# RWKV-7 units of a two-layer decoder trunk: state as a block-diagonal tile, triangular inverse from 64x64 tiles, uninterrupted r and v products

## The chip, the cores and the metric

The kernel runs on one core of a Trainium2 chip. The metric is device time in microseconds, as the median of the timed runs. All times of a trace are microseconds from the start of the span of one profiled execution, durations of single instructions are also given in ns. PE is TensorE, DVE is VectorE, ACT is ScalarE, POOL is GpSimd, SP is the queue that issues most DMAs.

## The reference, cut to what matters

A trunk of two layers on 256 tokens of 1024 features. The first layer is RWKV-7 time mixing and a dense SwiGLU; the second is dilated attention and a mixture of eight experts. The change touches only the time mixing. There, each of 16 heads carries a state of 64x64, and the recurrence over the tokens is

```python
def step(state, inp):
    r_t, w_t, k_t, v_t, a_t, b_t = inp
    sa = jnp.einsum('bhvk,bhk->bhv', state, a_t)
    state = state * w_t[:, :, None, :] + sa[..., None] * b_t[:, :, None, :] + v_t[..., None] * k_t[:, :, None, :]
    return state, jnp.einsum('bhvk,bhk->bhv', state, r_t)
```

with `r`, `k`, `v` from projections of the modulated input, and a per-head norm, a bonus term and a gate behind it, then the output projection `w_out`. Everything is float32.

## The kernel before, in words

**Chunks and units.** The 256 steps of the recurrence are cut into four chunks of 64 tokens. Within a chunk the recurrence becomes matrix products and the inverse of a 64x64 triangular matrix per head; between chunks only the state goes on. A *unit* (function `unit`, line 866) is one token tile of 128 tokens (two chunks, called `ch`) and four heads, so there are eight units: `c_` is the group of four heads, `t` the token tile. Four *lanes* hold the tiles of four units at a time, and each lane has one PSUM bank of its own (`lps`, line 880). The unit of `t = 1` needs the state that the unit of `t = 0` of the same heads leaves.

**What a unit does, in order.** Decay, keys and their norms (from line 908); transposes into `ART`, `BKn`, `BKT`; products that give `SM`, where `SM[:, ch, h, 0:64]` is what the inverse starts from; the inverse `E` (from line 1016); the chunk loop (from line 1089); head norm, bonus, gate and a transpose into `yg`, which the output projection reads.

**The inverse.** It doubles the block size at each of four levels (2, 4, 8, 16): product of `SM` with `T`, copy of it to `X` on ACT, product of `X` with `E`, a predicated copy into `E` on DVE, and a 32x32-blocked transpose of `E` into `T` on DVE. The two chunks lie in partitions 0 to 63 and 64 to 127. So that one product serves both chunks, `SM` is copied into `SMA`, a tile of 128x128 per head with the two 64x64 blocks on its diagonal, and `X` is such a tile too; POOL sets the other blocks to zero, and ACT writes the two blocks in two copies. A last level works on 32x32 tiles.

**The chunk loop.** For each chunk: `U` from `SM` times `SV` plus `ART` times the state; `E` times `U` into `SV`; the new state from `BKn` and `SV`, scaled by `PC` on DVE; `Y` from `SM` times `SV` plus `ART` times the state. The state is a tile `[128, 2, 64]`: of a pair of heads, one lies in partitions 0 to 63, the other in 64 to 127, so the product with the state is one of 64 rows of weights for each head, and the products with `SM` (128 rows of weights) and with the state alternate head by head.

**r and v.** `rv_task` (line 1189) makes r and v of four heads in *pieces*: four row chunks, two token tiles, and three products (`mm3`, line 452) for each, 24 products in all. There are 16 pieces. It hands control back ahead of every triple.

**What sets the order.** The order of the instructions on PE, DVE, ACT and POOL is written out by a planner (`spin`, line 1320): every task yields the engine and the tiles that its next instructions need, and the planner, by its own estimates of costs, always issues the one that can begin first. Between two yields nothing else is put. `keep_clock` (line 1358) adds products of nothing (`identr`) where the planner's ledger of columns says that PE does too little. All engine instructions pass through one helper, so all carry its line, L190; groups are told apart by tile names. On each engine they then run in the order written. Two further tasks run beside the units on ACT and POOL: rows of the adaLN weights are scaled (`rawa`) and summed (`acc`).

Of the kernel before, what the change touches and what calls it, by code (L numbers as in the profile page):

```python
# [33 lines left out]
S = 256  # L34
# [7 lines left out]
RANK0 = 1000                                              # ranks count from -RANK0  # L42
# [49 lines left out]
def tile_kernel(ctx: ExitStack, tc: tile.TileContext, cst_d, att_d, x, c, ada_w, ada_b, ln_g, ln_b, mu, w_rkv,  # L92
# [18 lines left out]
    def load(t_, src):  # L111
        """a large load into a tile of a ring"""
        n = 1
        for d_ in t_.shape:
            n *= d_
        k = t_.tensor.name
        clk["DMA"] = max(clk["DMA"], free.get(k, 0.0)) + n * 4 / 360
        rdy[k] = clk["DMA"] + 2000
        (nc.gpsimd if k in by_gp else SY).dma_start(t_, src)
# [5 lines left out]
    past = []                                              # when columns went through the tensor engine, and how many  # L125

    class Engine:
        """an engine, with an estimate of the time of every instruction, by which the units are interleaved"""
# [43 lines left out]
        def __getattr__(self, op):  # L172
            fn = getattr(self.real, op)

            def call(*a, **kw):
# [3 lines left out]
                for r in aps:  # L179
                    start = max(start, rdy.get(r.tensor.name, 0.0))  # L180
                    if r.tensor.name[:3] in ("psb", "mmb") and self.nm != "PE":    # one engine after the other
                        start = max([start] + [v for k, v in psr.get(r.tensor.name, {}).items() if k != self.nm])
# [49 lines left out]
    def raw_at(j, shape):  # L232
        """the place's tile, or its two tiles of half the size"""
# [9 lines left out]
    def raw_load(rws, src, rows_=None):  # L243
        """src: [128, k, n]"""
# [10 lines left out]
    def raw_tiles(kk, n):  # L255
        """for one load: a place, or two places of half the size, which are used once"""
# [34 lines left out]
    tl = cp.tile([128, 1], F32, name="tl")                # has the table of the next functions loaded  # L291
# [11 lines left out]
    # ---- adaLN vectors  # L303
    mods = {}

    def ada_end(idx, ps):
        """ps[g * 32]: a quarter of the vector"""
# [13 lines left out]
    def ada_pe(idx, get_raw, get_ps, n):  # L321
        """one adaLN vector; mods[idx][p, k] = vector[k * 128 + p]. Four groups of columns of the tensor engine
        each sum a quarter of the columns"""
# [17 lines left out]
    def ada_sum(idx, acc, get_ps):  # L341
        """sum over the partitions"""
# [15 lines left out]
    def ada_task(idx):  # L358
        """background work: one adaLN vector, chunk by chunk"""
# [17 lines left out]
    def ada_lane(idx):  # L377
        """the same beside the units"""
# [40 lines left out]
    def bcast_steps(idx, o, get_ps):  # L419
        """mods[idx] along the free axis, the same on every partition"""  # L420
# [17 lines left out]
    # ---- small helpers  # L438
# [21 lines left out]
    def wstream(w, K, n0, n, fine=False):  # L460
        """yield (k, hi, lo) for every 128 rows of w[:K, n0:n0+n]; fine: the last load by row chunks"""
# [15 lines left out]
    def proj2(xh, xl, w, K, n0, n, first=False, mid=()):  # L477
        """two token tiles, n <= 512 columns; first: all of token tile 0 before token tile 1"""
# [21 lines left out]
    def proj_wide(xh, xl, w, K, last=4, stream=None, mid=(), late=None):  # L500
        """[256, K] @ [K, 1024]; the last few row chunks finish token tile 0 before token tile 1"""
# [26 lines left out]
    def ln_rsqrt(var):  # L528
        """sqrt(1 / (var + eps)) per partition"""
# [14 lines left out]
    def pn_norm(t, yps, gate1, u, sc=()):  # L544
        """u = normalised sum of the residual and the gated branch, of token tile t; yps[half]: [128, 512]"""
# [26 lines left out]
    def pn_mod(t, u, mods, get_ps, get_tmp):  # L572
        """mods: (A, B, sink(t, hf, tmp)) per modulated copy, transposed"""
# [18 lines left out]
    def pn_res(t, u, gb, bb, eng):  # L592
        """the new residual"""
# [26 lines left out]
    # =====================================================================================  # L620
    # layer 0: RWKV-7
    # =====================================================================================
    up = rw_stack.enter_context(tc.tile_pool(name="up", bufs=2, reuse_waits="tile"))       # units
# [50 lines left out]
    # Work is cut into tasks, which are interleaved. A task yields what its next instructions begin with:  # L674
    # (engine, tiles read) or a condition to wait for.
# [6 lines left out]
    def loader():  # L682
        """weights, two tiles ahead"""
# [94 lines left out]
    def rvvar_task(i):  # L778
        """the variants of x for r and v, hi and lo"""
# [13 lines left out]
    # low-rank branches, first stage (transposed outputs)  # L793
# [43 lines left out]
    # units of one token tile (two chunks of 64) and four heads; a lane holds the tiles of one unit.  # L837
# [5 lines left out]
    def row_tiles(c_):  # L843
        """the broadcast rows of four heads"""
# [21 lines left out]
    def unit(i, lane):  # L866
# [25 lines left out]
        def newton(v, nm):  # L892
            """sqrt(1 / v)"""
# [18 lines left out]
        # decay, in-context rate a = (1 + tanh) / 2, keys; the sigmoids enter by their tanh  # L912
# [17 lines left out]
        # k2 = 2 * k * (1 + (a - 1) * k_a)  # L930
# [85 lines left out]
        # E = transpose of the inverse of (1 - strictly lower part of A B), by doubling the block size  # L1016
# [5 lines left out]
        SMA = lt("SMA", "BS", (128, 4, 128))  # L1022
        yield GP,
        halves(lambda sl, ch: GP.memset(SMA[sl, :, 64 - ch * 64:128 - ch * 64], 0.0))
        yield SC, SM
        halves(lambda sl, ch: SC.copy(SMA[sl, :, ch * 64:ch * 64 + 64], SM[sl, ch, :, 0:64]))
        X = lt("X", "t34", (128, 4, 128))
        yield GP,
        halves(lambda sl, ch: GP.memset(X[sl, :, 64 - ch * 64:128 - ch * 64], 0.0))
# [7 lines left out]
        for b in (2, 4, 8, 16):  # L1037
            yield PE, SMA, T
            ps = lps((128, 4, 64))
            for h in range(4):  # L1040
                PE.matmul(ps[:, h], SMA[:, h], T[:, h], start=True, stop=True)
            yield SC, ps
            halves(lambda sl, ch: SC.copy(X[sl, :, ch * 64:ch * 64 + 64], ps[sl]))
            yield PE, X
            ps = lps((128, 4, 64))
            for h in range(4):
                PE.matmul(ps[:, h], X[:, h], E[:, h], start=True, stop=True)
# [7 lines left out]
        for ch in range(2):  # L1055
            s0, s1 = slice(ch * 64, ch * 64 + 32), slice(ch * 64 + 32, ch * 64 + 64)
            for h in range(4):
# [8 lines left out]
        for ch in range(2):  # L1066
            s0, s1 = slice(ch * 64, ch * 64 + 32), slice(ch * 64 + 32, ch * 64 + 64)
            for h in range(4):
# [20 lines left out]
        # chunk after chunk; U = E'(A S + (strictly lower part of A K) V), its place in SV holds zeros before  # L1089
        Y = l4("Y", "t5")  # L1090
        for ch in range(2):
            sl = slice(ch * 64, ch * 64 + 64)
            yield lambda: ST_n.get(c_, 0) >= t * 2 + ch
            st = ST.get(c_)
            for par in range(2):
                hs = slice(par * 64, par * 64 + 64)
                yield PE, SV
                ps = lps((128, 2, 64))
                for pr in range(2):
                    h = pr * 2 + par  # L1100
                    PE.matmul(ps[sl, pr], SM[:, ch, h, 0:64], SV[:, ch, h * 64:(h + 1) * 64], start=True,
                              stop=st is None)
                    if st is not None:
                        PE.matmul(ps[sl, pr], ART[hs, pr, ch, 0], st[hs, pr], start=False, stop=True)
                yield SC, ps
                SC.copy(U[sl, par::2], ps[sl])
# [6 lines left out]
            if not (t == 1 and ch == 1):  # L1113
                yield PE, SV
                ps2 = lps((128, 2, 64))
                for h in range(4):
                    pr, hs = h // 2, slice((h % 2) * 64, (h % 2) * 64 + 64)
                    PE.matmul(ps2[hs, pr], BKn[:, ch, h * 64:(h + 1) * 64], SV[:, ch, h * 64:(h + 1) * 64],
                              start=True, stop=True)
                yield V, ps2  # L1120
                sn = up.tile([128, 2, 64], F32, name=f"ST{c_ % 2}_{ch}", bufs=1)
                pcb = PC[:, :, ch:ch + 1].to_broadcast([128, 2, 64])
                if st is None:
                    V.tensor_tensor(sn, ps2, pcb, op=OP.mult)
                else:
                    V.tensor_tensor(sn, ps2, st, op=OP.add)
                    yield V, sn
                    V.tensor_tensor(sn, sn, pcb, op=OP.mult)
                ST[c_] = sn
                ST_n[c_] = t * 2 + ch + 1  # L1130
            for par in range(2):
                hs = slice(par * 64, par * 64 + 64)
                yield PE, SV
                ps = lps((128, 2, 64))
                for pr in range(2):
                    h = pr * 2 + par
                    PE.matmul(ps[sl, pr], SM[:, ch, h, 64:128], SV[:, ch, h * 64:(h + 1) * 64], start=True,
                              stop=st is None)
                    if st is not None:
                        PE.matmul(ps[sl, pr], ART[hs, pr, ch, 1], st[hs, pr], start=False, stop=True)  # L1140
                yield SC, ps
# [1104 lines left out]
```

## Time and profile before

| what | value |
|---|---|
| median of three timed runs | 1970.92 us (1966.15, 1970.92, 1975.42) |
| span of the profiled execution | 1977.1 us |
| what the profile gives for that execution beside its span | nothing; the span itself stands 6.2 us above the median |
| instructions | 25695 |
| busy share of PE, DVE, ACT, POOL | 94%, 77%, 60%, 21% |
| mean granted TensorE clock | 0.915 |

One of the 40 slices of the page is 49.4 us. The units run from about 103 us to 495 us, in slices 3 to 10; the dense SwiGLU follows until about 705 us, attention until about 960 us, and the experts fill the rest. A group's "busy" is the union of its instructions' durations. [...] A float32 product leaves two records, each with its own load of weights; a product of the split weights (`whi`, `wlo`) leaves one.

### The profile page before, as it was taken

The page shows a single profiled execution, that of the slowest core. Times are in us where ns is not written, and L with a number is a line of the kernel's source. Part 1 is how long each engine was busy: PE and PEld are TensorE (multiplying, and loading weights), DVE is VectorE, ACT ScalarE, POOL GpSimd, SP SyncE. Part 2 cuts the span into 40 slices and gives each one's busy share as a digit, 9 for nine tenths or more (in the row PEclk, how much of TensorE's full clock was granted, in tenths as well). Part 3 has the DMA queues.
Part 4 walks back from the last instruction along what each step waited for, and adds up shares of the span by engine and source line. Part 5 has one row for each costly group of instructions (what it writes and reads, how often), then busy time and mean ns, then how long its engine had stood idle before and what let it go on. Part 6 is the DMA issues. An engine that isn't in the chain of part 4 may idle for free. (4 is left out here: it accounts for less than half of the span.)

```text
span 1977.1 us, 25695 instructions
## 1 busy us (share of the span) xinstructions
PE 1861.9 (94%) x9345; PEld 1491.3 (75%) x9345; DVE 1527.9 (77%) x2033; ACT 1184.5 (60%) x1592; POOL 408.3 (21%) x333
## 2 busy tenths in 40 slices
PE   5889999999999978898899999999999999999996
PEld 2478778887687866666788888888878878788775
DVE  3893347444798776786889989898898888988888
ACT  2354344333455536663678777787777777777764
POOL 2743324230345237753100000000000000000110
PEclk8895558559899989998999999999999999999998
DMA  8542213212498946654789999999999999999990
GB/s 279 153 139 64 67 57 98 92 64 72 165 331 305 332 143 234 232 192 174 294 299 344 364 348 347 376 343 364 337 349 353 355 350 337 354 348 355 342 318 25
DMA packets 213562, 498.89 MB, mean 252 GB/s; under 512 B 14634, under 2 KB 28818, under 8 KB 213428
## 3 DMA queue, kind: packets, MB, share of 16 engines
q1 hardware_dynamic: 212564, 494.03, 70.3%
q0 software_dynamic: 864, 3.15, 0.4%
q8 instruction: 75, 1.23, 0.3%
q14 instruction: 59, 0.48, 0.1%
HBM read 496.07 MB, written 1.06 MB: 251 GB/s over the span
## 5 line engine op out<-in xcount | busy, mean ns | idle before, releaser
L190 DVE TENSOR_TENSOR wlo<-raw,whi 128x1024 fp32r<-128x1024 f32 x804 | 999.7, 1281 | 144.2 <-ACT whi L190 130.2
L190 ACT CAST whi<-raw 128x1024 fp32r<-128x1024 f32 x812 | 828.1, 1048 | 263.3 <-PE mmb L190 207.0
L190 PE MATMUL mmb<-wlo,xeh 128*128 128x512 f32 x896 | 356.4, 398 | 4.9 <-DVE wlo L190 4.1
L190 PE MATMUL mmb<-whi,xeh 128*128 128x512 f32 x896 | 353.1, 395 | 0.0
L190 PE MATMUL mmb<-whi,xel 128*128 128x512 f32 x896 | 351.8, 393 | 0.0
L190 PEld LDWEIGHTS mmb<-wlo,xeh 128*128 128x128 f32 x896 | 168.7, 188 | 47.1 <-DVE wlo L190 13.4
L190 POOL TENSOR_TENSOR macc<-macc,gate 128x1024 f32<-128x1024 f32 x2 | 5.7, 2890 | 925.3 <-ACT gate L190 925.3
L190 PEld LDWEIGHTS mmb<-whi,xeh 128*128 128x128 f32 x896 | 168.6, 188 | 34.3 <-ACT whi L190 0.2
L190 PEld LDWEIGHTS mmb<-whi,xel 128*128 128x128 f32 x896 | 168.7, 188 | 32.7
L190 PE MATMUL psb<-wlo,ah 128*128 128x512 f32 x448 | 176.6, 394 | 1.5 <-DVE wlo L190 1.5
L190 PE MATMUL psb<-whi,al 128*128 128x512 f32 x448 | 174.8, 390 | 0.0
L190 PE MATMUL psb<-whi,ah 128*128 128x512 f32 x448 | 161.9, 392 | 0.0
L190 POOL TENSOR_TENSOR acc<-acc,raw 128x512 f32<-128x512 f32 (+1 forms) x62 | 128.2, 2082 | 75.6 <-DVE acc L190 44.2
L190 POOL TENSOR_TENSOR acc<-acc,rawa 128x512 f32<-128x512 f32 x56 | 74.2, 1330 | 142.2 <-ACT rawa L190 81.2
L190 PEld LDWEIGHTS psb<-wlo,ah 128*128 128x128 f32 x448 | 84.1, 188 | 24.7 <-DVE wlo L190 6.2
L190 PEld LDWEIGHTS psb<-whi,ah 128*128 128x128 f32 x448 | 83.5, 188 | 18.8 <-ACT whi L190 1.6
L190 PEld LDWEIGHTS psb<-whi,al 128*128 128x128 f32 x448 | 84.1, 188 | 16.5
L190 PE MATMUL mmb<-whi,f_xl 128*128 128x512 f32 (+1 forms) x192 | 72.5, 378 | 2.1 <-DVE f_xl L190 2.1
L190 PE MATMUL mmb<-whi,f_xh 128*128 128x512 f32 (+1 forms) x192 | 73.0, 381 | 0.0
L190 PE MATMUL mmb<-wlo,f_xh 128*128 128x512 f32 (+1 forms) x192 | 72.5, 377 | 0.2 <-DVE wlo L190 0.2
L190 ACT CAST ah<-psb 128x512 fp32r<-128x512 f32 x56 | 32.7, 583 | 61.0 <-PE psb L190 60.8
L190 ACT COPY X<-psb 64x256 f32<-64x256 f32 (+1 forms) x80 | 27.5, 344 | 64.1 <-PE psb L190 63.0
(415 smaller groups left out, 3048.3 us busy)
## 6 DMA issues: line engine op xcount, KB each, us to landing
raw<-in_moe_w_gu_dram SPq DMA_DIRECT2D x192, 1024.0 KB, 6.5
raw<-in_moe_w_down_dram SPq DMA_DIRECT2D x83, 1024.0 KB, 6.1
raw<-in_moe_w_gu_dram SPq DMA_DIRECT2D x60, 512.0 KB, 7.0
raw<-in_moe_w_down_dram SPq DMA_DIRECT2D x56, 512.0 KB, 6.1
raw<-in_ada_w_dram SPq DMA_DIRECT2D x42, 512.0 KB, 5.2
rawa<-in_ada_w_dram SPq DMA_DIRECT2D x40, 512.0 KB, 3.6
raw<-in_ada_w_dram SPq DMA_DIRECT2D x15, 1024.0 KB, 7.2
raw<-in_rw_w_rkv_dram SPq DMA_DIRECT2D x24, 512.0 KB, 3.7
```

The lines of the kernel that those rows point to most:

```text
L190: return fn(*a, **kw)
```

## The change

In the inverse, `SMA` and the wide `X` go. Each of the eight 64x64 matrices of a level (four heads, two chunks) is a product of its own, by the helper `mm64` that was there already, in the order head by head with the two chunks alternating; `X` is written in one copy. In the last level the two loops change places, so that the chunks alternate there too.

The state becomes `[128, 2, 128]`: of each pair of heads a 128x128 tile with the heads' states on the diagonal and zeros elsewhere. POOL makes `pcm`, the decay of the chunk in that layout with zeros off the diagonal (a memset and two copies for each unit), and DVE scales with it. The product with the state is one for each pair, and follows all four products with `SM`. `U` and `Y` come out in one copy each. The state of the first chunk lies in the lane's tile `t1`, that of the second in a tile of its own. The wait for the state of the unit before stands behind the four products with `SM`, no longer ahead of them.

In `rv_task` the 24 products of a piece follow one another with no yield between them.

The rest of the diff removes comments. Its core:

```diff
-        SMA = lt("SMA", "BS", (128, 4, 128))
-        yield GP,
-        halves(lambda sl, ch: GP.memset(SMA[sl, :, 64 - ch * 64:128 - ch * 64], 0.0))
-        yield SC, SM
-        halves(lambda sl, ch: SC.copy(SMA[sl, :, ch * 64:ch * 64 + 64], SM[sl, ch, :, 0:64]))
-        X = lt("X", "t34", (128, 4, 128))
-        yield GP,
-        halves(lambda sl, ch: GP.memset(X[sl, :, 64 - ch * 64:128 - ch * 64], 0.0))
...
         for b in (2, 4, 8, 16):
-            yield PE, SMA, T
+            yield PE, SM, T
             ps = lps((128, 4, 64))
-            for h in range(4):
-                PE.matmul(ps[:, h], SMA[:, h], T[:, h], start=True, stop=True)
+            mm64(ps, lambda sl, ch, h: SM[sl, ch, h, 0:64], lambda sl, ch, h: T[sl, h])
             yield SC, ps
-            halves(lambda sl, ch: SC.copy(X[sl, :, ch * 64:ch * 64 + 64], ps[sl]))
+            X = l4("X", "t1")
+            SC.copy(X, ps)
             yield PE, X
             ps = lps((128, 4, 64))
-            for h in range(4):
-                PE.matmul(ps[:, h], X[:, h], E[:, h], start=True, stop=True)
+            mm64(ps, lambda sl, ch, h: X[sl, h], lambda sl, ch, h: E[sl, h])
...
+        pcm = lt("pcm", "t34", (128, 2, 2, 128))
+        yield GP, PC
+        GP.memset(pcm.rearrange("p c r n -> p (c r n)"), 0.0)
+        halves(lambda sl, par: GP.tensor_copy(
+            pcm[sl, :, :, par * 64:par * 64 + 64],
+            PC[sl].rearrange("p r c -> p c r").unsqueeze(3).to_broadcast([64, 2, 2, 64])))
+
+        def with_state(ps, sl, ch, a, st):
+            for pr in range(2):
+                PE.matmul(ps[sl, 2 * pr:2 * pr + 2].rearrange("p h n -> p (h n)"), ART[:, pr, ch, a], st[:, pr],
+                          start=False, stop=pr == 1)
...
-            for par in range(2):
-                hs = slice(par * 64, par * 64 + 64)
-                yield PE, SV
-                ps = lps((128, 2, 64))
-                for pr in range(2):
-                    h = pr * 2 + par
-                    PE.matmul(ps[sl, pr], SM[:, ch, h, 0:64], SV[:, ch, h * 64:(h + 1) * 64], start=True,
-                              stop=st is None)
-                    if st is not None:
-                        PE.matmul(ps[sl, pr], ART[hs, pr, ch, 0], st[hs, pr], start=False, stop=True)
-                yield SC, ps
-                SC.copy(U[sl, par::2], ps[sl])
+            for h in range(4):
+                PE.matmul(ps[sl, h], SM[:, ch, h, 0:64], SV[:, ch, h * 64:(h + 1) * 64], start=h == 0,
+                          stop=first and h == 3)
+            st = None
+            if not first:
+                yield lambda: ST_n.get(c_, 0) >= t * 2 + ch
+                st = ST[c_]
+                yield PE, st
+                with_state(ps, sl, ch, 0, st)
+            yield SC, ps
+            SC.copy(U[sl], ps[sl])
...
-                ps2 = lps((128, 2, 64))
-                for h in range(4):
-                    pr, hs = h // 2, slice((h % 2) * 64, (h % 2) * 64 + 64)
-                    PE.matmul(ps2[hs, pr], BKn[:, ch, h * 64:(h + 1) * 64], SV[:, ch, h * 64:(h + 1) * 64],
-                              start=True, stop=True)
+                ps2 = lps((128, 2, 128))
+                for pr in range(2):
+                    prs = slice(pr * 128, (pr + 1) * 128)
+                    PE.matmul(ps2[:, pr], BKn[:, ch, prs], SV[:, ch, prs], start=True, stop=True)
...
+            yield lambda: xvn[i] > q * 4 + 3
+            yield PE, hi, lo, xl, ps[0], ps[1]
             for k in range(4):
                 kk = q * 4 + k
                 for t in range(2):
-                    yield lambda: xvn[i] > kk
-                    yield PE, hi, lo, xl, ps[t]
```

More of the change, by code (lines that the diff above doesn't have):

```diff
@@ L1054, in unit @@
         ps = lps((128, 4, 32))
-        for ch in range(2):
-            s0, s1 = slice(ch * 64, ch * 64 + 32), slice(ch * 64 + 32, ch * 64 + 64)
-            for h in range(4):
+        for h in range(4):
+            for ch in range(2):
+                s0, s1 = slice(ch * 64, ch * 64 + 32), slice(ch * 64 + 32, ch * 64 + 64)
                 PE.matmul(ps[s1, h], SM[s0, ch, h, 32:64], T[s0, h, 0:32], start=True, stop=True,
@@ L1065, in unit @@
         ps = lps((128, 4, 32))
-        for ch in range(2):
-            s0, s1 = slice(ch * 64, ch * 64 + 32), slice(ch * 64 + 32, ch * 64 + 64)
-            for h in range(4):
+        for h in range(4):
+            for ch in range(2):
+                s0, s1 = slice(ch * 64, ch * 64 + 32), slice(ch * 64 + 32, ch * 64 + 64)
                 PE.matmul(ps[s0, h], X[s1, h, 0:32], E[s1, h, 32:64], start=True, stop=True,
@@ L1090, in unit @@
         Y = l4("Y", "t5")
+        pcm = lt("pcm", "t34", (128, 2, 2, 128))
[8 more added lines that the diff above has]
+                          start=False, stop=pr == 1)
         for ch in range(2):
             sl = slice(ch * 64, ch * 64 + 64)
-            yield lambda: ST_n.get(c_, 0) >= t * 2 + ch
-            st = ST.get(c_)
-            for par in range(2):
-                hs = slice(par * 64, par * 64 + 64)
-                yield PE, SV
-                ps = lps((128, 2, 64))
-                for pr in range(2):
-                    h = pr * 2 + par
-                    PE.matmul(ps[sl, pr], SM[:, ch, h, 0:64], SV[:, ch, h * 64:(h + 1) * 64], start=True,
-                              stop=st is None)
-                    if st is not None:
-                        PE.matmul(ps[sl, pr], ART[hs, pr, ch, 0], st[hs, pr], start=False, stop=True)
-                yield SC, ps
-                SC.copy(U[sl, par::2], ps[sl])
+            first = t == 0 and ch == 0
+            yield PE, SV
+            ps = lps((128, 4, 64))
+            for h in range(4):
+                PE.matmul(ps[sl, h], SM[:, ch, h, 0:64], SV[:, ch, h * 64:(h + 1) * 64], start=h == 0,
[8 more added lines that the diff above has]
+            SC.copy(U[sl], ps[sl])
             yield PE, U
@@ L1114, in unit @@
                 yield PE, SV
-                ps2 = lps((128, 2, 64))
-                for h in range(4):
-                    pr, hs = h // 2, slice((h % 2) * 64, (h % 2) * 64 + 64)
-                    PE.matmul(ps2[hs, pr], BKn[:, ch, h * 64:(h + 1) * 64], SV[:, ch, h * 64:(h + 1) * 64],
-                              start=True, stop=True)
-                yield V, ps2
-                sn = up.tile([128, 2, 64], F32, name=f"ST{c_ % 2}_{ch}", bufs=1)
-                pcb = PC[:, :, ch:ch + 1].to_broadcast([128, 2, 64])
@@ L1123, in unit @@
-                if st is None:
-                    V.tensor_tensor(sn, ps2, pcb, op=OP.mult)
-                else:
+                ps2 = lps((128, 2, 128))
+                for pr in range(2):
+                    prs = slice(pr * 128, (pr + 1) * 128)
+                    PE.matmul(ps2[:, pr], BKn[:, ch, prs], SV[:, ch, prs], start=True, stop=True)
+                yield V, ps2
+                sn = lt("ST", "t1", (128, 2, 128)) if ch == 0 else up.tile([128, 2, 128], F32, name=f"ST{c_ % 2}",
+                                                                                   bufs=1)
@@ L1126, in unit @@
+                if st is not None:
                     V.tensor_tensor(sn, ps2, st, op=OP.add)
                     yield V, sn
-                    V.tensor_tensor(sn, sn, pcb, op=OP.mult)
+                V.tensor_tensor(sn, ps2 if st is None else sn, pcm[:, ch], op=OP.mult)
                 ST[c_] = sn
                 ST_n[c_] = t * 2 + ch + 1
[L1131 to L1141, printed above, removed]
-                SC.copy(Y[sl, par::2], ps[sl])
+            yield PE, SV
@@ L1144, in unit @@
+            ps = lps((128, 4, 64))
+            for h in range(4):
+                PE.matmul(ps[sl, h], SM[:, ch, h, 64:128], SV[:, ch, h * 64:(h + 1) * 64], start=h == 0,
+                          stop=first and h == 3)
+            if not first:
+                with_state(ps, sl, ch, 1, st)
+            yield SC, ps
+            SC.copy(Y[sl], ps[sl])
         yield GP, v_, bon
```

## The prediction

> **What bounds the kernel now.** I read the page's slices first, then the engines' busy time by stage, then the waits of the units' stage, then its timeline on PE. On the page, PE's busy tenths and the granted clock:
>
> ```profile
> PE   5889999999999978898899999999999999999996
> PEclk8895558559899989998999999999999999999998
> ```
>
> PE is at 9 and over in slices 4 to 6, 8 and 9 while its clock is at about half. So the clock, not idle time, marks the stage. The stretches of the units (length; busy time with count of PE, PEld, DVE, ACT, POOL; clock; DMA share; GB/s):
>
> ```profile
> 151.00:291.00 140.00, 139.35 (x766) 114.96 (x766) 48.20 (x146) 54.46 (x132) 41.70 (x51) 0.51 0.20 60
> 291.00:349.00 58.00, 54.94 (x390) 46.72 (x390) 43.77 (x121) 29.34 (x69) 22.37 (x29) 0.86 0.34 105
> 349.00:435.00 86.00, 85.79 (x444) 72.64 (x444) 41.05 (x116) 29.75 (x72) 27.62 (x33) 0.51 0.22 73
> 435.00:495.00 60.00, 59.56 (x423) 43.54 (x423) 29.98 (x75) 22.19 (x51) 5.39 (x11) 0.99 0.24 80
> ```
>
> They hold two cold stretches, 140 + 86 = 226 us, in which PE is never free, the clock is 0.51, DVE and ACT are busy under half the time and DMA under a quarter. There PE's work is time, one for one. In 291 to 349 DVE is busy 43.77 of 58 us, so PE does not bound that stretch alone. The waits from 125 to 495 agree: the others wait for PE.
>
> ```profile
> DVE E L190 <- PE psb L190: 67.0, 26, 7.1
> ACT X L190 <- PE psb L190: 63.0, 30, 5.3
> ```
>
> Nothing behind the stage has a start of its own: DMA stands at 0.24 when the stage ends, and the dense layer's loads wait for buffers that the units hold. So I take what is won by 495 as won at the end.
>
> **The change part by part.** Prices come from starts on PE's timeline, at half clock:
>
> ```profile
> 199.66 1.97 PE L190 MATMUL psb<-E,X 128*128 128x64 f32 x8
> 201.55 1.11 PE L190 MATMUL psb<-U,E 64*64 64x64 f32 x8
> 202.59 0.58 PE L190 MATMUL mmb<-whi,x2h 128*128 128x256 f32 x1
> 202.97 0.41 PE L190 MATMUL mmb<-wlo,x2h 128*128 128x256 f32 x1
> ...
> 204.81 0.70 PE L190 MATMUL psb<-SV,BKn 128*64 128x64 f32 x8
> 205.44 1.97 PE L190 MATMUL psb<-T,SMA 128*128 128x64 f32 x8
> 207.17 0.56 PE L190 MATMUL mmb<-whi,x2h 128*128 128x256 f32 x1
> ...
> 208.09 0.48 PE L190 MATMUL psb<-SV,SM 128*64 128x64 f32 x2
> ...
> 211.31 0.47 PE L190 MATMUL psb<-E,X 128*128 128x64 f32 x1
> ```
>
> and at full clock:
>
> ```profile
> 445.67 0.68 PE L190 MATMUL psb<-U,E 64*64 64x64 f32 x8
> 446.27 1.10 PE L190 MATMUL psb<-T,SMA 128*128 128x64 f32 x8
> 447.31 0.45 PE L190 MATMUL psb<-SV,BKn 128*64 128x64 f32 x8
> 447.69 0.50 PE L190 MATMUL mmb<-whi,ygh 128*128 128x512 f32 x1
> ...
> 478.53 0.33 PE L190 MATMUL psb<-SV,SM 128*64 128x64 f32 x2
> ...
> 479.04 0.33 PE L190 MATMUL psb<-SV,SM 128*64 128x64 f32 x2
> ```
>
> How much of each kind lies in the first and in the second cold stretch (records by form; busy, mean ns):
>
> ```profile
> L190 PE MATMUL psb<-E,X 128*128 128x64 f32 x104 | 25.5, 427 | 0.0
> L190 PE MATMUL psb<-ST,ART 64*64 64x64 f32 x72 | 17.1, 339 | 0.0
> L190 PE MATMUL mmb<-whi,x0h 128*128 128x256 f32 x13 | 6.4, 491 | 0.0
> L190 PE MATMUL mmb<-whi,x2h 128*128 128x256 f32 x9 | 4.5, 505 | 0.0
> ...
> L190 PE MATMUL psb<-E,X 128*128 128x64 f32 x56 | 13.0, 421 | 0.2 <-ACT X L190 0.2
> L190 PE MATMUL psb<-ST,ART 64*64 64x64 f32 x48 | 11.4, 339 | 0.0
> L190 PE MATMUL mmb<-whi,x2h 128*128 128x256 f32 x16 | 8.2, 515 | 0.0
> L190 PE MATMUL mmb<-whi,x0h 128*128 128x256 f32 x5 | 2.4, 484 | 0.0
> ```
>
> *Inverse.* One of its products for four heads leaves 8 records and costs 1.73 us (205.44 to 207.17) to 1.89 us (199.66 to 201.55) cold, 1.04 warm (446.27 to 447.31). Afterwards it is 8 products in alternating quadrants, 16 records. No such pair is in the trace. Its bounds: U,E, one quadrant throughout, leaves 8 records in 1.04 cold and 0.60 warm, so 16 cost at most 2.08 and 1.20; SV,BKn, which alternates the two column halves, leaves 8 in 0.63 and 0.38, so 16 cost 1.26 and 0.76 with two entries, less with one. I take 1.1 and 0.65, by SV,BKn, the nearer kind: its neighbouring products share no cell of the array either. There are 8 units x 4 levels x 2 = 64 such groups. Of E,X 104 + 56 = 160 records are cold, 20 groups; T,SMA comes once for each, so 40 are cold and 24 not. Cold: 40 x (1.8 - 1.1) = 28 us off; elsewhere 24 x 0.39 = 9 off. At the other bound it is 40 x 0.28 = 11 and 24 x 0.16 = 4 more instead.
>
> *U and Y.* Four heads with the state cost 3.22 cold (208.09 to 211.31) and four times 0.51 = 2.04 warm (478.53 to 479.04 is one head), since each head goes from 128 rows of weights to 64 and back. Afterwards there are four products with SM in a row, priced as U,E, and two of 128 columns with the state, 4 records, for which I take these, of 128x128 weights and 128 columns, as nearest:
>
> ```profile
> 434.85 1.89 PE L190 MATMUL mmb<-cst,mod 128*128 128x128 f32 x8
> 436.58 0.67 PE L190 MATMUL psb<-E,X 128*128 128x64 f32 x5
> ```
>
> 1.73 / 8 = 0.216 each cold, half that warm. New: 1.04 + 0.86 = 1.90, and 0.60 + 0.43 = 1.03. Twenty-four groups have the state, of which (72 + 48) / 8 = 15 are cold: 15 x 1.32 = 20 off; elsewhere 9 x 1.01 = 9 off. If the SM products went at the pace of column halves (0.63), 26 off; if they kept 0.40 a pair, 15 x 0.76 = 11.
>
> *Pieces.* A product that follows other work costs 0.38 (202.59 to 202.97), against 0.21 inside a run. The mean durations of the first of a triple, 484 to 515 ns, stand some 0.09 over the 0.41 of the second. With 13 + 9 + 16 + 5 = 43 triples cold that is 4 us, of which one entry in eight stays: 3 off.
>
> *Small PE items.* The state product of BKn becomes 4 records of 0.216 in place of 8 in 0.63: 9 times 0.23, 2 more. The last level's alternation can at best halve a group of 32x32 products; 1.5 off.
>
> Cold sum: 28 + 20 + 3 - 2 + 1.5 = 50. Elsewhere 9 + 9 = 18, of which I count half, as DVE shares that time: 9. Together **59**.
>
> *The clock.* In 291 to 349 it comes back after runs of r and v products:
>
> ```profile
> 313.60:317.00 3.40, 3.40 (x16) 3.22 (x15) 3.29 (x5) 0.94 (x1) 3.27 (x5) 0.50 0.00 0
> 317.00:320.40 3.40, 3.16 (x25) 2.82 (x25) 3.32 (x11) 2.87 (x9) 0.07 (x1) 1.00 0.58 168
> ...
> 429.70:433.10 3.40, 3.40 (x18) 3.40 (x18) 2.05 (x5) 1.76 (x4) 1.31 (x2) 0.50 0.00 0
> ```
>
> For all but the first half microsecond of the first row PE runs such products alone, and in the next row it has 1.00. In the third row it runs inverse products for most of the time, as busy, and stays at 0.50; the run of nine r and v products from 202.59 to 204.81 was too short. A whole piece is 24 x 0.21 = 5.1 us at half clock, longer than the first row. The cold stretches hold 43 / 8 = 5 pieces. Lower bound: each brings one stretch of 3.4 us at full clock, in which PE does what takes 6.8 cold: 17 us. Upper: all of 226 - 50 = 176 us runs warm, 88. The stretch 291 to 349, whose clock is 0.86 on the mean, is nearer the upper, but its PE work was lighter and the cold came back at 349. I take a little under the middle: **45**.
>
> *What comes back.* Once PE is no longer the sole bound, a unit that wants PE inside a piece waits for it: 2.9 us a piece at full clock, half on the mean, 16 pieces, 23 us if always on the path; while PE is full it costs nothing. I take 16. On DVE and POOL:
>
> ```profile
> L190 DVE TENSOR_TENSOR ST<-psb,ST x8: 278/291/292, 205.6 to 466.8; 128x128 f32<-128x128 f32 x8
> L190 POOL MEMSET X<- x16: 304/306/319, 128.7 to 401.4; 64x256 f32 x16
> ```
>
> Some 20 operations on the state double in size (0.29 to about 0.42): 3 us on the chain from unit to unit. POOL loses 32 memsets of 0.306 (10 us) and gets three instructions a unit, by size about 2 us, 16 in all, under its 41.70 busy of 140; with no cover each unit would be those 2 us late. ACT's paired copies of U, X and Y become single ones, hidden by PE as long as it is full; I count the rest of this as 1 back. Sum back: **20**.
>
> 1977.1 - 59 - 45 + 20 = 1893 us of span. The median of the runs stands 6.2 under this span: **1887**.
>
> **The rivals.**
>
> *A. Warm throughout.* Once warm, the denser U and Y groups and the pieces keep the clock up, and all 176 us run at full clock: 59 + 88 - 20 = 127 off, 1844. For it: after 435, with output products between the units', the clock is 0.99. Against it: inverse work ran cold from 349 on, and the inverse stays.
>
> *B. Quadrants don't overlap.* The inverse then takes 11 us more cold and 4 elsewhere, so the PE sum is 20 + 3 - 2 + 1.5 - 11 + (9 - 4) / 2 = 14; with the clock's lower bound and 8 back that is 23 off, 1948. For it: no 64x64 pair is in the trace, and U,E in one quadrant goes no faster for its work than the 128x128 tile. Against it: SV,BKn's 0.63 for eight. [...]
>
> *C. POOL holds the state.* The decay tile stands in POOL's fixed order, and each scaling on DVE, with all that is queued behind it there, waits for it. Waits that POOL has now:
>
> ```profile
> POOL acc L190 <- ACT rawa L190: 81.2, 19, 11.2
> POOL Y L190 <- DVE Y L190: 71.0, 8, 24.5
> ```
>
> Behind one like POOL Y's (8.9 us on the mean, 24.5 at most) a unit's state is late by as much. The gain of 84 is gone at 84 / 8 = 10.5 us for each of the eight units; at 13 it gives 1991. Against it: the memsets of SV, right before the tile in the same queue, are needed earlier in the unit already.
>
> *D. Nothing to speak of.* The planner's new order eats what PE gains: 1970. Against it: PE is never free for 226 us.
>
> **How the numbers follow.** Forecast 0.47, A 0.23, B 0.17, C 0.08, D 0.05. 0.5% is about 10 us, what a measurement can tell from no change: faster 0.87, same 0.05, slower 0.08. The forecast's own range is 1850 to 1920; with A below and B above, 1830 to 1945 holds 8 in 10.
>
> **What would show it.** Right: 16 records of an inverse group within 1.3 us cold; no 64-row products with the state; 24 r and v products in one run, followed by clock 1.00; cold stretches of under 130 us together; DVE's share of the stage up. Wrong: inverse groups at 2 us cold (B); DVE waiting for POOL at the state (C); half clock for over 150 us although PE has less to do; a units' stage that ends after 450.

## The result, and the profile after

The changed kernel takes 1895.8 us (median of six runs, 1893.0 to 1905.1) against 1973.2 us before (median of six): a ratio of 0.961, with a 95% interval of 0.957 to 0.965. Forecast were 1887 us, with a range of 1830 to 1945. The profiled execution of the changed kernel took 1905.1 us, with a span of 1902.9, so 2.2 us lie around the span. Ratios and medians, here and in the experiments, leave out slow executions: six of before in two of the later sets, and one of 2010.0 us of the inverse alone with the ledger's line.

All of the difference is made before the units end. The last write of the units' output, one row of the group by tile before and one after (min/median/max ns, then first and last start):

```profile
L190 DVE TENSOR_TENSOR ygl<-psb,ygh x8: 411/424/426, 243.5 to 494.8; 128x256 fp32r<-128x256 f32 x8
```

```profile
L190 DVE TENSOR_TENSOR ygl<-psb,ygh x8: 414/423/425, 220.1 to 421.9; 128x256 fp32r<-128x256 f32 x8
```

The units end 72.9 us earlier, the span 74.2; what follows the units took 1482.3 us before and 1481.0 after. So what is won in the stage does come out at the end.

The stages of the changed kernel over the same stretches (length; busy PE, PEld, DVE, ACT, POOL; clock; DMA share; GB/s), to be read against the first table of the prediction:

```profile
115.00:151.00 36.00, 34.69 (x271) 31.14 (x270) 32.03 (x93) 22.98 (x52) 9.16 (x8) 1.00 0.45 140
151.00:291.00 140.00, 123.39 (x1369) 99.02 (x1369) 105.11 (x295) 65.80 (x152) 66.37 (x75) 0.80 0.34 105
291.00:349.00 58.00, 44.92 (x559) 36.85 (x558) 35.24 (x101) 30.06 (x69) 36.26 (x43) 0.71 0.36 110
349.00:435.00 86.00, 83.13 (x508) 58.69 (x507) 46.43 (x111) 20.67 (x38) 16.35 (x17) 0.80 0.18 56
```

In 151 to 291 the clock went from 0.51 to 0.80 and DVE's busy time from 48.20 to 105.11 us (146 and 295 instructions): on DVE, about twice the work fits into the same time. But between 291 and 349 PE is free for 13 us and the clock is lower than before. The stage is no longer full of PE, and half clock is not gone: added up from the record of the granted clock, from 103 us to the end of the units, 242 us before and 117 after.

### The profile page after: what moved, and what is told of

The parts are those of the page before. It is cut to its first block, busy times and chain, and to the rows that moved or that the text cites. A ratio compares the mean times of both kernels' runs of the same rounds, so it can differ in the third digit from the quotient of the medians.

```text
span 1902.9 us, 26448 instructions
## 1 busy us (share of the span) xinstructions
PE 1766.8 (93%) x9763; PEld 1406.8 (74%) x9763; DVE 1526.9 (80%) x2032; ACT 1160.3 (61%) x1512; POOL 413.5 (22%) x326
## 5 line engine op out<-in xcount | busy, mean ns | idle before, releaser
L190 ACT ACTIVATE e_s<-mmb 128x512 f32<-128x512 f32 x56 | 33.5, 599 | 44.8 <-PE mmb L190 44.8
```

The costliest lines, as they stand in the source:

```text
L190: return fn(*a, **kw)
```

## The experiments

All were compared with the kernel before, run beside them in four sets; its median was 1969.2 to 1973.5 us in each, so medians of different sets are also compared with one another. Of the columns behind the ratio, which are read from each run's one trace, "half clock" is that sum from 103 us to the last write to `ygl`, "fillers" are the records of `identr` (products of nothing) in that time, with their busy time, and "early" is how many of the 128 triples of r and v began before 151 us. One trace is one execution, and executions of one kernel differ: the inverse alone ran from 1950.3 to 1977.1 us at mean clocks of 0.940 to 0.920, and its trace is of the longest.

| kernel | median us | ratio, 95% interval | units end | half clock us | fillers | early |
|---|---|---|---|---|---|---|
| before | 1973.2 | | 494.8 | 242 | 55, 14 us | 55 |
| changed | 1895.8 | 0.961, 0.957 to 0.965 | 421.9 | 117 | 107, 36 us | 96 |
| inverse alone | 1963.7 | 0.996, 0.991 to 1.001 | 493.6 | 205 | 213, 69 us | 53 |
| state alone | 1918.4 | 0.973, 0.965 to 0.981 | 431.6 | 130 | 76, 20 us | 55 |
| pieces alone | 2013.5 | 1.021, 1.013 to 1.028 | 528.7 | 310 | 93, 35 us | 96 |
| state and pieces | 1953.4 | 0.993, 0.990 to 0.995 | 470.8 | 220 | 82, 28 us | 96 |
| inverse and state | 1875.5 | 0.954, 0.947 to 0.961 | 388.7 | 34 | 118, 33 us | 54 |
| changed, quadrants in rows | 1916.6 | 0.972, 0.964 to 0.979 | 432.1 | 135 | 92, 30 us | 96 |
| changed, no fillers | 1885.9 | 0.959, 0.954 to 0.964 | 406.1 | 98 | 0 | 68 |
| changed, ledger | 1876.4 | 0.954, 0.949 to 0.959 | 393.2 | 70 | 93, 27 us | 74 |
| changed, pieces after the low-rank branches | 1901.0 | 0.961, 0.954 to 0.967 | 415.6 | 83 | 158, 54 us | 64 |
| inverse alone, ledger | 1895.0 | 0.961, 0.952 to 0.971 | 414.2 | 112 | 54, 17 us | 58 |
| inverse and state, no fillers | 1878.1 | 0.950, 0.944 to 0.955 | 393.3 | 80 | 0 | 36 |
| inverse and state, ledger | 1855.2 | 0.938, 0.932 to 0.943 | 377.1 | 53 | 57, 20 us | 58 |

Two things run through the table. The time behind the units' end is 1476 to 1483 us in every trace, so only the stage matters. And the time goes with the half clock: the kernels sort nearly alike by both. By itself that does not say which is the cause, as a longer stage has more of both; and the fastest kernel has 53 us, the next 34.

### The three edits, each alone

**The inverse alone.** Only the hunks on `SMA`, `X`, `mm64` and the last level's loops.

```diff
-            for h in range(4):
-                PE.matmul(ps[:, h], SMA[:, h], T[:, h], start=True, stop=True)
+            mm64(ps, lambda sl, ch, h: SM[sl, ch, h, 0:64], lambda sl, ch, h: T[sl, h])
```

> The kernel before with the inverse edit alone (64x64 products in alternating quadrants, no SMA, X in one copy, last level's loops swapped). Theory of the prediction: the inverse's term, 28 us in the cold stretches and 9 elsewhere, of which half on the path, so 33 us off, ratio 0.983; inverse groups of 16 records cost about 1.1 us cold. Rival that quadrants don't overlap: groups of 2.0 us and a time within 10 us of before or above it. Rival that the clock is all: the groups are cheaper, but the stretches stay at 0.5 and the gain is under 15 us.

Measured: 1963.7 us, a ratio of 0.996 whose interval holds 1. Yet the groups themselves are as cheap as forecast. The trace's matmul records overlap: in before, eight of `psb<-T,SMA` span 1.97 us from 205.44, and the next product starts after 1.73. So costs are taken from one start to the next. On PE's timeline of this kernel, one group at half clock and, a little later, what stands beside such groups:

```profile
179.42 1.12 PE L190 MATMUL psb<-T,SM 64*64 64x64 f32 x16
180.47 0.69 PE L190 MATMUL psb<-SV,SM 128*64 128x64 f32 x4
...
186.10 2.50 PE L190 MATMUL mmb<-identr 128*128 128x256 f32 x6
188.54 1.11 PE L190 MATMUL psb<-U,E 64*64 64x64 f32 x8
189.58 0.79 PE L190 MATMUL mmb<-identr 128*128 128x256 f32 x2
```

Sixteen records of the inverse take 1.05 us; eight of U,E in one quadrant still take 1.04. But six fillers take 2.4 us right there. The fillers from 103 to 430 us, first before, then in this kernel (length; busy PE, PEld and DVE with counts; clock; DMA share; GB/s):

```profile
103.00:430.00 327.00, 8.04 (x25) 4.51 (x25) 0.00 (x0) 0.64 0.27 84
```

```profile
103.00:430.00 327.00, 59.02 (x177) 35.72 (x177) 0.00 (x0) 0.69 0.29 87
```

Of the three theories on record the third is nearest: the groups are cheap and the gain is under 15 us. But the clock did not stay at 0.5 throughout (0.57, 0.50 and 0.64 in the three stretches from 151 to 300 us), and none of the three had the products of nothing, which went from 8 to 59 us of PE here.

**The state alone.** The hunks of the chunk loop, with `pcm` and `with_state`.

```diff
-                    if st is not None:
-                        PE.matmul(ps[sl, pr], ART[hs, pr, ch, 0], st[hs, pr], start=False, stop=True)
+            if not first:
+                with_state(ps, sl, ch, 0, st)
```

> The kernel before with the state edit alone (block-diagonal state, four SM products in a row, pcm on POOL). Theory of the prediction: 20 us off in the cold stretches, 4 or 5 elsewhere, 3 or 4 back on DVE and POOL, so 20 us off, ratio 0.99; a U or Y group costs 1.9 us cold instead of 3.2, and DVE does not wait for POOL at the state. Rival that POOL holds the state: DVE waits for pcm show up, and the time does not fall. Rival that the denser groups also lift the clock: more than 35 us off.

Measured: 55 us off, ratio 0.973, more than twice what was expected; half clock falls from 242 to 130 us. A group with the state costs what was expected, 1.90 us at half clock (217.36 to 219.26):

```profile
217.36 1.11 PE L190 MATMUL psb<-SV,SM 128*64 128x64 f32 x8
218.27 1.06 PE L190 MATMUL psb<-ST,ART 128*64 128x128 f32 x4
219.26 0.58 PE L190 MATMUL mmb<-whi,x2h 128*128 128x256 f32 x1
```

So the last rival on this list has the time and the half clock right. That it is the density of the groups that lifts the clock fits the count at the end of this text; no run parts it from what else the state edit changes (single copies, a later wait, another order by the planner). DVE does not wait for POOL at the state: there, all its idle time that the trace gives (10.3 us) ended with PE. In the changed kernel, too, the rows by tile show what DVE's and POOL's part costs, and of the decay tile as a whole only this is in the list of waits:

```profile
L190 POOL COPY pcm<-PC x16: 389/399/1182, 181.7 to 378.7; 64x256 f32<-64x256 f32 x16
L190 POOL MEMSET pcm<- x8: 529/530/531, 181.1 to 376.9; 128x512 f32 x8
L190 DVE TENSOR_TENSOR ST<-ST,pcm x8: 381/416/1227, 197.8 to 398.0; 128x256 f32<-128x256 f32 x8
...
DVE ST L190 <- PE psb L190: 6.2, 6, 1.8
...
DVE ST L190 <- POOL acc L190: 0.3, 1, 0.3
```

**The pieces alone.**

```diff
+            yield lambda: xvn[i] > q * 4 + 3
+            yield PE, hi, lo, xl, ps[0], ps[1]
             for k in range(4):
                 kk = q * 4 + k
                 for t in range(2):
-                    yield lambda: xvn[i] > kk
-                    yield PE, hi, lo, xl, ps[t]
```

> The kernel before with uninterrupted r and v pieces alone. Theory of the prediction: entries 3 us, the clock's term between 17 and 88 us with 45 taken, some 10 back since units wait inside pieces: about 38 us off, ratio 0.98, with the granted clock of the units' stage up from 0.66 to 0.75 or more. Rival that only PE's own work counts: 3 us off, no change that can be told, clock as before. Rival that pieces only hold the units up: 10 to 20 us more than before.

Measured: 40 us *slower*, ratio 1.021. My clock theory fails outright: half clock rises from 242 to 310 us. Neither rival holds: one had no change, the other 10 to 20 us more. Where the v products lie, by the records that read `x2l` (one a triple), first before, then with the pieces alone (length; busy PE, PEld and POOL with counts; clock; DMA share; GB/s):

```profile
103.00:151.00 48.00, 6.88 (x23) 4.80 (x23) 0.14 (x1) 0.96 0.43 137
151.00:289.00 138.00, 3.73 (x9) 2.97 (x9) 0.00 (x0) 0.51 0.19 60
289.00:349.00 60.00, 5.09 (x16) 3.73 (x16) 0.00 (x0) 0.85 0.34 105
349.00:435.00 86.00, 6.64 (x16) 5.28 (x16) 0.00 (x0) 0.51 0.22 73
```

```profile
103.00:151.00 48.00, 11.27 (x40) 7.63 (x40) 1.46 (x1) 1.00 0.47 147
151.00:289.00 138.00, 0.00 (x0) 0.00 (x0) 0.00 (x0) 0.52 0.21 64
289.00:349.00 60.00, 4.50 (x16) 3.04 (x16) 0.00 (x0) 0.73 0.42 132
349.00:435.00 86.00, 0.00 (x0) 0.00 (x0) 0.00 (x0) 0.50 0.16 49
```

Uninterrupted, the planner issues twelve of the sixteen pieces ahead of 151 us, at full clock, and the rest in one clump at 289. Two stretches of 138 and 86 us hold none, and run at half clock but for the first 7 us of the first. The first step of the inverse begins at 156.6 us instead of 136.9, as the products of the low-rank branches come after pieces.

### How the edits meet

**State and pieces, without the inverse.** The hunks of both, as above.

> The state edit and the uninterrupted pieces, with the inverse of before. Tells what the inverse edit is worth beside the others. Theory 1, PE's price: without it the units' stage is 20 to 40 us longer than in the changed kernel, 1915 to 1935. Theory 2, the products of nothing that the ledger adds for 64x64 tiles eat it, as in the run of the inverse alone, which gained 8 us: within 10 us of the changed kernel. Theory 3, the pieces hurt here as they did alone: above 1945.

**Inverse and state, without the pieces.**

> The inverse and the state edit without the third: r and v products yield ahead of every triple, as before. Alone, the uninterrupted pieces made the kernel 40 us slower. Theory 1, pieces take the dense products away from the rest of the units' work, whatever else is there: this is 20 to 40 us faster than the changed kernel, near 1865. Theory 2, with the state edit the rest is dense enough by itself, and the pieces then only save their entries and their half-clock time: this is 5 to 25 us slower than the changed kernel, 1900 to 1920. The singles' sum for these two (8 and 55 us off) gives 1910.

Measured: 1953.4 and 1875.5 us; of the theories on record the third holds for the one, and for the other the first, at its lower end. Adding the pieces costs 35 us on top of the state, 40 on nothing, and 20 on top of inverse and state. Adding the inverse brings 8 us on nothing, which cannot be told from none, but 43 on top of the state and 58 on top of state and pieces. The version without the pieces is 20 us faster than the changed kernel, at 34 us of half clock.

**Pieces after the low-rank branches.** The changed kernel with the first piece held back.

```diff
+        done["lora"] = 1
         yield lambda: xvn[0] == xvn[2] == 8
...
-        yield lambda: len(ksb) == 2
+        yield lambda: len(ksb) == 2 and done.get("lora")
```

> The changed kernel, in which the first uninterrupted piece waits until the low-rank branches are done. In the changed kernel 12 of 16 pieces run before 150 us, and the first inverse begins at 153 instead of 137 us. Theory 1, the pieces hurt by pushing the units' start back: the start returns to about 140 and the time falls by 10 to 16 us. Theory 2, they hurt by leaving no dense products for the middle of the stage: the start returns, and the time stays within 5 us of the changed kernel.

Measured: the inverse starts at 140.2 instead of 152.9 us, and the time, 1901.0, cannot be told from the changed kernel's. So the first theory, a late start that costs 10 to 16 us, fails. The second has the time, 5 us from the changed kernel, but this run does not test its reason: half the triples lie behind 151 us here, and half clock falls to 83 us, while fillers rise from 36 to 54 us of PE. How the pieces' loss divides between clumps of dense products, units that wait for a clump and the fillers that come with them stays open.

### Overlap, fillers and the ledger

**Quadrants in rows.** The changed kernel with the loops of `mm64` turned round, so that four neighbours share a quadrant.

```diff
-            for h in range(4):
-                for ch in range(2):
+            for ch in range(2):
+                for h in range(4):
```

> The changed kernel with the order of the 64x64 products in the inverse turned round: all four heads of one chunk, then all four of the other, so that neighbouring products lie in the same quadrant. If the overlap of neighbouring quadrants is what makes the groups cheap, 16 records cost 2.0 us cold and 1.1 warm instead of about 1.1 and 0.65, and the 64 groups add 64 x 0.45 to 0.9 us of PE work, 29 to 58 us, of which the part counts where PE is the bound: 10 to 40 us slower than the changed kernel. If the queue finds the overlap by itself over a longer reach, or if the chain and not PE bounds the stage now, it is within 5 us of the changed kernel.

Measured: 1916.6 us, 21 more than the changed kernel. A group now lasts from 159.35 to 160.88, 1.53 us, at half clock and from 188.65 to 189.54, 0.89 us, at full clock in this kernel:

```profile
159.35 1.60 PE L190 MATMUL psb<-E,X 64*64 64x64 f32 x16
160.88 2.07 PE L190 MATMUL psb<-ART,BKT 64*128 64x128 f32 x8
...
188.65 0.96 PE L190 MATMUL psb<-T,SM 64*64 64x64 f32 x16
189.54 0.66 PE L190 MATMUL psb<-cst,BKn 128*128 128x128 f32 x4
```

and in the changed kernel 0.61 us at full clock and 1.05 at half:

```profile
169.46 1.12 PE L190 MATMUL psb<-E,X 64*64 64x64 f32 x16
170.51 0.58 PE L190 MATMUL mmb<-identr 128*128 128x256 f32 x1
...
188.50 0.68 PE L190 MATMUL psb<-E,X 64*64 64x64 f32 x16
189.11 0.71 PE L190 MATMUL psb<-SV,BKn 128*128 128x128 f32 x4
...
191.63 0.65 PE L190 MATMUL psb<-SV,SM 128*64 128x64 f32 x8 [0.18 <-ACT Y L190]
192.12 0.60 PE L190 MATMUL psb<-ST,ART 128*64 128x128 f32 x4
192.65 1.05 PE L190 MATMUL psb<-E,X 64*64 64x64 f32 x32
```

So in these two kernels products in different quadrants overlap, and the order matters: 0.28 us in 64 groups is 18 us, 0.48 us at half clock would be 31. That these make the 21 us is not shown alone: turned round, the products no longer alternate, so the planner also counts them in full, and by itself that count makes the changed kernel 19 us faster (the ledger, below). Even in rows a group, at 0.89 us, is under the 1.20 us of two runs in one quadrant at full clock (twice 445.67 to 446.27 in before), so some overlap is found across four products as well. The products of the two chunks write different partitions of one lane's bank, and overlap there: in turn, 16 records take 1.05 us at half clock where 8 in one quadrant take 1.04 (188.54 to 189.58 with the inverse alone).

**No fillers**, in the changed kernel and in the one without pieces.

```diff
     def keep_clock(at):
+        return
```

> The changed kernel without the products of nothing that the planner puts into the units' stage. They hold PE for some 36 us there. Theory 1, they only cost, since PE is full where they stand: 15 to 30 us faster than the changed kernel. Theory 2, they keep the clock up in the inverse: more half clock (mean clock of the units' stage under 0.75) and 10 to 40 us slower.

> Inverse and state edits with yielding triples, and no products of nothing in the units' stage. Theory 1, with dense products spread over the stage the fillers (45 us of PE there) only cost: 10 us or more faster than the same with fillers, below 1866. Theory 2, that kernel stays warm by its fillers (34 us of half clock): without them the half clock comes back, over 80 us of it, and the time is 1885 or more.

Measured: 1885.9 and 1878.1 us. In the changed kernel the fillers cost 10 us net, less than expected, and half clock is not more without them (98 us against 117). The order changes with them, though: 68 triples are early instead of 96. Without the pieces they cost nothing that can be told (1875.5 with, 1878.1 without), though half clock goes from 34 to 80 us: what they take from PE and what they give to the clock may then be about even, but here, too, the order changes (36 early triples instead of 54). Neither theory had that.

**The ledger.** The planner counts a 64x64 product that alternates by half of its rows' share.

```diff
-                    ham["n"] += passes * n * k / (128 if not alt else 256 if m > 32 else 512)
+                    ham["n"] += passes * n * k / 128
```

> The changed kernel with one line of the planner's ledger changed: products of 64 and 32 rows and columns that alternate count by their rows like all others, not a half or a quarter of it. The trace of the changed kernel switches the clock at about 3000 columns by rows in 3.4 us, with the alternating ones counted that way. Theory: the planner then puts in fewer products of nothing (56 + 46 to less than half), without losing the clock: 5 to 20 us faster than the changed kernel. Rival: the missing products cost the clock, 5 to 20 us slower.

> The kernel before with the inverse edit alone and the ledger's line changed. The inverse alone saved 45 us of its own PE time and gained 8, with 223 products of nothing where before had 61. Theory 1, the ledger's low count of 64x64 tiles makes those fillers, which eat the gain: with the line changed there are under 100 and the time is 1930 to 1945. Theory 2, the fillers come from PE being free earlier, whatever the count: as many as before, and within 10 us of the inverse alone.

> Inverse and state edits with yielding r and v triples, and the ledger's line changed. The two steps gave 20 and 19 us alone against the changed kernel. Theory 1, both work by keeping the clock up, of which the first leaves only 34 us at half clock: together they give little over the first, 1865 to 1880. Theory 2, they work by different means and add up: 1850 to 1862.

Measured: 1876.4, 1895.0 and 1855.2 us. With the inverse alone the line makes 69 us and brings the fillers from 213 to 54: the first theory there, and more than it asked. Half clock falls there, too, from 205 to 112 us. What the line does to the kernel before, without any edit, was not run. Fillers from 103 to 430 us with it, to be read against the 59.02 above:

```profile
103.00:430.00 327.00, 24.83 (x85) 15.63 (x85) 0.00 (x0) 0.82 0.33 102
```

In the changed kernel the reason on record was wrong: the 19 us came with about as many fillers (93 against 107). What differed is the order: 74 early triples instead of 96, the first step of the inverse at 142.5, half clock 70 us. The same line changes what the planner takes the clock and so the costs to be; which part of that did it was not separated. With inverse and state it makes 20 us more and gives the fastest kernel, 1855.2 us, 0.938 of before (0.932 to 0.943). There the two steps add up, as the second theory on record had it.

## Why the prediction was right, and where it was wrong

The sum was near (1887 against 1895.8), and the place: the two stretches at half clock, and nothing behind the units. But it came out near by luck, as terms missed in opposite ways. On record for the state, the inverse and the pieces alone were 20, 33 and 38 us off. Put in one after the other, in this order, they made 55 and 43 us off and 20 us back (1973.2, 1918.4, 1875.5, 1895.8).

**Prices on PE: right.** A group of the inverse was put at 1.1 us cold and 0.65 warm; it costs 1.05 and 0.61. A group with the state was put at 1.90 cold and 1.03 warm; it costs 1.90 (217.36 to 219.26) and 1.02 (191.63 to 192.65). Within it the products with `SM` cost less than was taken (0.91 and 0.49 for 1.04 and 0.60), those with the state more (0.99 and 0.53 for 0.86 and 0.43). The prediction put the old price down to the change between 128 rows of weights and 64: at half clock two records with `SM` took 0.40 when they alternated with the state's (208.09 to 208.49 in before), and take 0.23 in a row (a quarter of the 0.91); no run parts the rows from the order. Rival B (no overlap) falls by the rows above.

**Inverse, 28 + 9 us: right as PE time, wrong as time won when alone.** The step assumed that PE time saved in a full stretch is won. Alone, what it saved was refilled with fillers, 69 us of them instead of 14, which the ledger's lower count of the new tiles called for; that the planner's own products answer to the change was not in the sum. Rival D, that the planner's order eats the gain, is what happened to this edit alone. With the ledger's line the edit stands 78 us under before; how much of that is the line's own is not known.

**U and Y, 20 + 9 us: too small.** The state edit alone made 55 us. The step counted the groups' own time, and gave the clock's return to the pieces instead. In the state run half clock falls by 112 us with the r and v products left as they were, so the clock came back without the pieces. That the groups themselves, of whose products every second one used half of the rows, had held it down is an inference from the count at the end.

**The clock, 45 us from the pieces: the wrong cause.** The clock did rise (242 to 117 us of half clock), but alone the pieces lowered it and cost 40 us, and taking them out of the changed kernel makes it 20 us faster. The step took from 313.60 to 320.40 that a run of dense products wakes the clock, which agrees with the last table (23 of 26 half-clock steps with a sum over 3300 were followed by full clock), and missed that each piece moved is a dense stretch taken from elsewhere: the planner put twelve of sixteen where the clock was full already. In the changed kernel the other four run from 227 to 245 us, where the clock is 1.00 as well: from 103 us on, no piece of it lies in a stretch at half clock, so there was none that it could wake (length; busy PE, PEld, DVE, ACT, POOL; clock; DMA share; GB/s):

```profile
227.00:245.00 18.00, 17.98 (x183) 15.65 (x184) 15.36 (x47) 7.38 (x18) 9.12 (x13) 1.00 0.51 161
```

**What comes back, 20 us: not found as such.** Units did not wait for the decay tile; rival C is out by the 0.3 us above. DVE's operations on the state cost 0.416 against the 0.42 taken. The 16 us for waits inside pieces were reckoned over sixteen pieces among the units; twelve ran ahead of the first inverse. The pieces did cost 20 us, by the run without them, but what share of it is waiting was not measured; the later start of the units is not it, as with that start 13 us earlier again the time stayed.

**The marks named.** Groups within 1.3 us cold, no products of 64 rows with the state, DVE's share up, and a stage that ends ahead of 450: as forecast. Runs of 24 products of r and v came, but at a clock of 1.00 before and during them, not as what brings it. Half clock of 117 us lies within the 130 given. Rival A, warm throughout, is no longer a rival of the changed kernel, but nearly describes the one without the pieces: 1844 was worked out for it, 1875 measured.

## What to carry to other kernels

Where TensorE is full at half clock, ask of each group of products how many columns it streams, weighted by the rows of weights it uses, in its time, and not only how long it takes: in the eight traces counted below, 261 of 262 half-clock steps with a sum under 3000 were followed by half clock, and here the merging of two 64-row operands into one of 128 rows brought 55 us where the time of the products alone gave 29 at most. Dense products may be worth spreading among sparse ones; here an edit that let a planner issue them in one go spent them where the clock was full already. And where a planner fills gaps by a count of its own, correct the count for a new kind of instruction before judging the edit.

## What was not expected of the hardware

In the traces of this case the granted clock goes with a count of the matmul records. In before and changed its record holds 1.00 and 0.50 alone, and every stretch but the last of each trace is a whole number of steps of 3.41 us (in before, 153.18 to 293.12 us at half clock are 41). I cut 150 to 420 us of eight traces (before, changed, the three edits alone, no pieces, no fillers, ledger) into such steps and summed each step's streamed columns, weighted by the rows of weights over 128, twice for a float32 product's record: at half clock one of 128 columns costs 0.216 us (434.85 to 436.58 in before, eight records), and one of 256 columns of split weights 0.21 (203.19 to 203.40). (The products of `acc` with `ones` count a quarter: they write four strips of 32 partitions in turn and overlap, eight records of 256 columns in 0.57 us at full clock, from 184.63 to 185.20 in the changed kernel, where products of 256 columns one after another take 0.12 each, eight from 317.08 to 318.02 in before.)

| clock in the step | sum in the step | steps | followed by full clock |
|---|---|---|---|
| full | under 3000 | 37 | 1 |
| full | 3000 and over | 276 | 275 |
| half | under 3000 | 262 | 1 |
| half | 3000 to 3300 | 24 | 10 |
| half | over 3300 | 26 | 23 |

So a bound of 3000, drawn from these steps, misses 20 of the 625. It is a count over traces: no run sets the sum and nothing else. Without the weight by rows the best bound misses 65. A quadrant product is counted here by its 64 rows, and of two that overlap both are: with those of the inverse counted at half, 40 are missed.

The largest sum of a step at half clock is 4096, as in the row of the prediction from 313.60 to 317.00, two float32 records of 256 columns and twelve split-weight ones (2 x 512 + 12 x 256). A stream of 128x128 float32 tiles against 64 columns, 16 records a step at 0.216 us each, makes 16 x 128 = 2048, half of that with PE as busy; the row from 429.70 to 433.10, inverse products for the most part, has 2432, and the step stays at half clock.

With the prices at half clock this count gives an estimate for each group, in a step of 3.41 us. A group of the inverse sums to 1024: in 1.8 us that is 1940 a step, in the new 1.05 us 3330, and in rows, in 1.53 us, 2280. A group with the state went from 1536 in 3.22 us, 1630 a step, to 2048 in 1.90 us, 3680. So by this estimate both edits lift their groups from below the bound to above it, which was in none of the terms of the prediction.
